# RWKV-7 chains of a hybrid diffusion layer: joins put between the steps of the preceding job's chain, states of two pairs updated side by side

## The chip, the cores and the metric

The kernel is one program on one core of one Trainium2 chip. Its engines are TensorE (PE, with its weight loads as PEld), VectorE (DVE), ScalarE (ACT), GpSimd (POOL) and SyncE (SP), which issues most of the DMAs. The metric is the device time in microseconds, and a lower one is better. Each engine works through its own list of instructions in order and waits on semaphores for the others.

## What is computed

The reference is one layer with two groups of heads. A chunkwise mLSTM and a bidirectional RWKV-7 read the same input projection, first for 256 context tokens and then for 512 latent tokens. The latent scans start from the context's final states. An output projection, a gated convolutional FFN and a norm follow.

```python
def rwkv7_scan(r, w, k, v, kk, a, s0, reverse):
    def step(s, xs):
        r_t, w_t, k_t, v_t, kk_t, a_t = xs
        s = (s * w_t[:, :, None, :]
             - jnp.einsum("bhvk,bhk->bhv", s, kk_t)[..., None] * (kk_t * a_t)[:, :, None, :]
             + v_t[..., :, None] * k_t[..., None, :])
        return s, jnp.einsum("bhvk,bhk->bhv", s, r_t)
...
y_f, s_f = rwkv7_scan(rh, hd(decay[:, :, 0]), ..., state[2], False)
y_b, s_b = rwkv7_scan(rh, hd(decay[:, :, 1]), ..., state[3], True)
```

There are 16 such heads of 64 channels, in two directions.

## The kernel before

**Stages.** First come the modulation vectors and the context tokens' input projection, done in parts. Then the latent tokens' input projection runs head by head: `x_first`, `x_pair(0)` to `x_pair(7)`, and the four `x_head`s. Then the output projection runs in two halves (`out_first` over channels whose inputs are ready early, then the rest), and the FFN follows. All projections are split into high and low parts: ACT writes `whi` (line 299), DVE writes `wlo` (line 300), and each tile of weights gives three matmuls (lines 370 to 372 for `proj`, 403 to 405 for `proj_tm`, 1266 to 1268 for the first half of the output projection).

**RWKV-7 in chunks.** Heads are handled as 8 pairs, and two pairs make a job: four jobs for the context (4 chunks of 64 tokens each) and four for the latent tokens (8 chunks each). I call the latent jobs A (pairs 0 and 1), B (2, 3), C (4, 5) and D (6, 7). A job goes through four parts:

- `prep` (lines 680 to 775), once per pair and direction for the latent tokens: decays, masked products of all chunks (`G`, line 750) and transposed keys (line 759), written to DRAM in `S_d`.
- `tsolve` (777 to 801): 60 operations on DVE, one after the other, that invert 32x32 triangular blocks.
- `tjoin` (803 to 827): joins these blocks to 64x64 ones. For each pair it loads `t_Y`, transposes on DVE (813), multiplies on PE (819), copies on ACT (821), multiplies again (824), copies on DVE (826) and stores. There is one buffer `t_Y`, so the second pair's load waits for the first pair's store. Its PSUM banks come from the pool "pre", which `prep` uses too.
- `chain` and `chain_step` (843 to 933): the recurrence over chunks, forward and backward for both pairs at once. That makes four units, each with a state `u.M` of 128x64. A step multiplies the values and the states with the chunk's matrices (line 868), copies the result to `r_Rs` on ACT (872), multiplies again (875, 878), copies to `r_U` on ACT (880), multiplies with that (884, 887), and then DVE makes the new states (892) and adds to the outputs `r_yt` (902, 904). All products of a step lie in two banks of the pool "R", which has two, so the next step's first products wait until DVE has read both.

**Order.** `x_job(p)` runs `prep` for pair p. If a job is solved it then joins it, if a job is joined it runs its chain, and after every second pair it solves the two just made. So the chain of A stands in `x_job(2)`, those of B and C in `x_job(4)` and `x_job(6)`, and D is joined and run through its chain behind the loop. Between two steps of a latent chain (at c = 2 and 6) `fin_step` takes up half a `finalize_pair`, the normalisation and gating of a pair whose chain is done. `ada_late` puts 4 MB chunks of the modulation weights through DVE (line 232). The mLSTM heads (`mlstm_head`) 0 to 2 use buffers of the pool `rp` that `prep`, `tsolve` and `tjoin` use as well (`t_X`, `r_Gp`, `r_KR`), so they can only start when the last pair's are free. This program order is a priority: the build reorders each engine's list by its own timeline, so that projections stand between the steps of the chains.

Of the kernel before, what the change touches and what calls it, by code (L numbers as in the profile page):

```python
# [96 lines left out]
def body(tc, A, dbg=None):  # L97
# [705 lines left out]
    def tjoin(pairs):  # L803

        nc_ = 2 * pairs[0][0].nch
        XT = rp("t_X", [P, 2, 16, 32], 1)
        for k, us in enumerate(pairs):
            kc = us[0].kc
            T_d = us[0].S_d[:, :, kc:kc + 64]
            T = rp("t_Y", [P, 16, 64], 1)[:, 0:nc_]  # L810
            sp.dma_start(T, T_d)
            W = XT[:, k, 0:nc_]
            dve.transpose(W, T[:, :, 0:32])
            ws = [PS("pre", [P, 16, 32])[:, 0:nc_] for _ in range(2)]
# [12 lines left out]
            sp.dma_start(T_d, T)  # L827

# [14 lines left out]
    def chain_step(units, first, last):  # L843
# [5 lines left out]
        opened = {}  # L849

# [12 lines left out]
        for src in (1, 0):  # L863
            for u, w, c, V, n in units:
                for j in range(2 if x else 1):
                    for h in range(2):
                        o = 2 * kc * src + 64 * j
                        mm(h, h if j == 0 else 1 - h, n, w[:, o:o + 64], V[:, c, :] if src else u.M)
# [4 lines left out]
        for u, w, c, V, n in units:  # L873
            for h in range(2):
                mm(h, 1 - h, 4 + n, w[:, kc:kc + 64], Rs[:, n, :])
            for h in range(2):
                if not last:
                    mm(h, h, 4 + n, w[:, 3 * kc + 64:3 * kc + 128], V[:, c, :])
        for h, hs in enumerate(LOHI):
            act.copy(U[hs], bank[h][LOHI[1 - h], 4:8, :])  # L880
        for u, w, c, V, n in units:
            for h in range(2):
                if not last:
                    mm(h, h, 4 + n, w[:, 3 * kc:3 * kc + 64], U[:, n, :])
# [3 lines left out]
        if not last:  # L888
            for u, w, c, V, n in units:
                g = u.g0 + c  # L890
                for h, hs in enumerate(LOHI):
                    dve.scalar_tensor_tensor(u.M[hs], u.M[hs], u.gC[hs, g:g + 1], bank[h][hs, 4 + n, :], ALU.mult, ALU.add)  # L892
        if x:
            for k in range(0, len(units), 2):
                cs = [units[k][2], units[k + 1][2]]
                lo, hi = min(cs), max(cs)
                y = units[k][0].y
                for h in range(2):
                    hs = LOHI[1 - h]
                    out = y[hs, lo:hi + 1:hi - lo, :]  # L900
                    if first:
                        dve.tensor_copy(out, bank[h][hs, k:k + 2, :])
                    else:
                        dve.tensor_tensor(out, bank[h][hs, k:k + 2, :], out, ALU.add)

    def chain(pairs, mid):
# [3 lines left out]
        Vs, ys = [], []  # L910
        for us in pairs:
            Vs.append(chain_v(us[0].p, us[0].seg, nch))
            ys.append(rk("r_yt", [P, 8, 64], 2) if x else None)
            for u in us:
                if not x:
                    Mst[(u.p, u.d)] = rk("r_M", [P, 64], 16)
                    pool.memset(Mst[(u.p, u.d)], 0.0)
                u.M = Mst[(u.p, u.d)]
        for c in range(nch):
            if x and c in (2, 6):  # L920
                mid()
            units = []
            for k, (us, V, y) in enumerate(zip(pairs, Vs, ys)):
                us[0].y = y
                for j, u in enumerate(us):
                    cu = nch - 1 - c if j else c
                    units.append((u, chain_load(u, cu), cu, V, 2 * k + (j if 2 * c < nch - 1 else 1 - j)))
            chain_step(units, c < nch // 2, x and c == nch - 1)
        if x:
            for us, y in zip(pairs, ys):  # L930
                y_d = us[0].y_d = DT("yr_d", [4, P, 128], 8)
                for h in range(2):
                    sp.dma_start(y_d[:, :, 64 * h:64 * h + 64].rearrange("a (b t) v -> t (a b) v", t=64), y[LOHI[1 - h]])

    def bonus(p, uf, ub, s):
# [8 lines left out]
        bo = rk("r_bo", [P, 8], 6)  # L944
# [69 lines left out]
    def ctx_part(H, k0, k1, part):  # L1014
        for n, (tag, (kind, *ts)) in enumerate(ctx_plan):
            if k0 == 0:
                if tag == "am":
                    if n % 2 == 0:
                        pair = am()
# [128 lines left out]

    def do_solve():
        job = list(made)  # L1150
        made.clear()
        tsolve([us for _, us, _ in job])
        solved.append(job)

    def ctx_job(p):
# [3 lines left out]
        do_join()  # L1159
        do_chain()  # L1160
        do_solve()

    def x_job(p):
# [4 lines left out]
        do_join()  # L1168
        do_chain()
        if p % 2:  # L1170
            do_solve()

# [69 lines left out]
    do_join()  # L1242
# [262 lines left out]
```

## Time and profile before

| what | value |
|---|---|
| time, median of 3 runs | 3369.24 us (3366.53 to 3373.36) |
| the profiled execution | 3371.52 us, its span 3369.7 us |
| PE busy | 3081.6 us (91%) |
| DVE busy | 2165.6 us (64%) |
| ACT busy | 1182.0 us (35%) |
| mean granted clock of TensorE | 0.938 |

The profile page gives busy times as shares of the whole span, which joins stages with different limits. So it is to be read by stages: from the table of stretches, which has one row per stretch with the busy time of each engine, the granted clock, the share of the DMA engines and what they moved. The FFN, from 1890 us on, is a stage of its own.

### The profile page before, as it was taken

The numbers are of one execution on the slowest core, as the hardware profiler recorded it, in microseconds if no ns is written. First come the engines' busy times: TensorE is split into PE (matmuls) and PEld (weight loads), VectorE is DVE, ScalarE is ACT, GpSimd is POOL, SyncE is SP. The second block draws the span as 40 slices with busy tenths as digits, with TensorE's granted clock in tenths as the row PEclk, the third lists the DMA queues.
The fourth block names the chain that finished last, engine by engine and source line by source line (L and its number), as shares of the span: only waits on it lengthen the run. The fifth ranks groups of instructions, "written<-read, shape, count | busy, mean of one in ns | idle before, by whom it ended". The sixth has DMA issues, their size and how long they took to land.

```text
span 3369.7 us, 54393 instructions
## 1 busy us (share of the span) xinstructions
PE 3081.6 (91%) x21030; PEld 2518.3 (75%) x21030; DVE 2165.6 (64%) x4178; ACT 1182.0 (35%) x2237; POOL 58.4 (2%) x113
## 2 busy tenths in 40 slices
PE   8998889898988989567898899999999999999998
PEld 5687777787876767445676688888888888888887
DVE  2578766669668796747744788455555555555657
ACT  4356444334343434214333432232222222322323
POOL 0000100000000000000000000000000000000000
PEclk9998998999998999567898999999999999999999
DMA  8877554558566868657844255232232232222232
GB/s 282 309 243 227 154 152 146 166 158 264 179 202 203 261 208 246 207 162 248 280 155 143 82 194 194 94 100 95 94 100 95 94 99 96 94 98 96 94 100 101
DMA packets 404114, 548.53 MB, mean 163 GB/s; under 512 B 153200, under 2 KB 274312, under 8 KB 403600
## 3 DMA queue, kind: packets, MB, share of 16 engines
q1 hardware_dynamic: 394208, 531.68, 49.7%
q10 hardware_dynamic: 9648, 13.37, 1.1%
q8 instruction: 166, 2.72, 0.3%
q14 instruction: 92, 0.75, 0.1%
HBM read 457.49 MB, written 87.47 MB: 162 GB/s over the span
## 4 chain that ended last, share of the span: by engine, by line
PE 48%; DMA 6%; DVE 5%; ACT 2%; issue 1%; SPq 1%; POOL 0%; DVEq 0%; ACTq 0%
PE acc L370 9%; PE acc L372 9%; PE acc L371 9%; PE acc L1380 5%; PE acc L1381 5%; PE acc L1382 5%; DMA am<-in_wmod 2%; PE acc L1266 1%; PE acc L1268 1%; PE acc L1267 1%; DVE adacc L232 1%; DMA x_d<-ev 1%; DMA wraw<-in_wdn 0%; DVE r_M L892 0%; PE R L861 0%
## 5 line engine op out<-in xcount | busy, mean ns | idle before, releaser
L299 ACT CAST whi<-wraw 128x512 fp32r<-128x512 f32 (+1 forms) x948 | 569.1, 604 | 1342.6 <-PE acc L371 701.8
L300 DVE TENSOR_TENSOR wlo<-wraw,whi 128x512 fp32r<-128x512 f32 (+1 forms) x948 | 626.8, 665 | 462.2 <-ACT whi L299 455.9
L372 PE MATMUL acc<-H,wlo 128*128 128x512 f32 x1920 | 757.2, 394 | 6.2 <-DVE wlo L300 6.2
L370 PE MATMUL acc<-H,whi 128*128 128x512 f32 x1920 | 760.2, 396 | 1.2 <-ACT upad L1321 0.5
L371 PE MATMUL acc<-H,whi 128*128 128x512 f32 x1920 | 755.5, 393 | 0.0
L372 PEld LDWEIGHTS acc<-H,wlo 128*128 128x128 f32 x1920 | 363.8, 189 | 85.7 <-DVE wlo L300 8.4
L370 PEld LDWEIGHTS acc<-H,whi 128*128 128x128 f32 x1920 | 363.3, 189 | 82.4 <-issue 3.6
L371 PEld LDWEIGHTS acc<-H,whi 128*128 128x128 f32 x1920 | 363.7, 189 | 77.9 <-issue 2.9
L1384 DVE SCALAR_TENSOR_TENSOR x<-acc,mod,x 128x512 f32<-128x512 f32 (+1 forms) x192 | 135.5, 706 | 222.0 <-PE acc L1382 222.0
L1328 DVE SCALAR_TENSOR_TENSOR f_cv<-upad,fvec,f_cv 128x512 f32<-128x512 f32 x352 | 263.5, 749 | 7.2
L1380 PE MATMUL acc<-fh,whi 128*128 128x512 f32 x640 | 253.2, 396 | 0.0
L1381 PE MATMUL acc<-fl,whi 128*128 128x512 f32 x640 | 253.1, 396 | 0.0
L1382 PE MATMUL acc<-fh,wlo 128*128 128x512 f32 x640 | 253.1, 396 | 0.0
L232 DVE SCALAR_TENSOR_TENSOR adacc<-am,csil,adacc 128x512 f32<-128x512 f32 x240 | 179.1, 746 | 45.9 <-DMA am<-in_wmod 43.5
L405 PE MATMUL acc<-wlo,H 128*128 128x256 f32 x512 | 155.0, 306 | 6.5 <-DVE wlo L300 6.5
L403 PE MATMUL acc<-whi,H 128*128 128x256 f32 x512 | 155.9, 305 | 3.1 <-ACT whi L299 3.1
L404 PE MATMUL acc<-whi,H 128*128 128x256 f32 x512 | 152.9, 299 | 0.0
L1382 PEld LDWEIGHTS acc<-fh,wlo 128*128 128x128 f32 x640 | 120.2, 188 | 29.1
L1381 PEld LDWEIGHTS acc<-fl,whi 128*128 128x128 f32 x640 | 120.2, 188 | 29.0
L1380 PEld LDWEIGHTS acc<-fh,whi 128*128 128x128 f32 x640 | 120.2, 188 | 29.0
L750 DVE TENSOR_TENSOR r_Gp<-pre,c_gmask 64x512 f32<-64x512 f32 (+1 forms) x192 | 115.1, 600 | 25.0 <-DMA Sx_d<-r_Gp 14.6
L1266 PE MATMUL acc<-H,whi 128*128 128x512 f32 x256 | 104.6, 413 | 22.4 <-ACT H L299 17.4
(350 smaller groups left out, 4686.5 us busy)
## 6 DMA issues: line engine op xcount, KB each, us to landing
am<-in_wmod SPq DMA_DIRECT2D x128, 512.0 KB
wraw<-in_wup SPq DMA_DIRECT2D x88, 512.0 KB
wraw<-in_wgate SPq DMA_DIRECT2D x88, 512.0 KB
wraw<-in_wdn SPq DMA_DIRECT2D x88, 512.0 KB
wraw<-in_wcm SPq DMA_DIRECT2D x72, 512.0 KB
r_GK<-Sx_d SPq DMA_DIRECT2D x128, 256.0 KB
wraw<-in_wtm SPq DMA_DIRECT2D x56, 512.0 KB
Sx_d<-r_Gp SPq DMA_DIRECT2D x32, 512.0 KB
```

Of the source, the lines that this page charges most:

```text
L232: dve.scalar_tensor_tensor(acc, wm[:, k % 2], csil[:, k:k + 1], acc, ALU.mult, ALU.add)
L299: act.copy(hi, t)
L300: dve.tensor_tensor(lo, t, hi.bitcast(F32), ALU.subtract)
L370: pe.matmul(pt[:, :n], hi(k8), H.h(k), start=k == 0, stop=False)
L371: pe.matmul(pt[:, :n], hi(k8), H.l(k), start=False, stop=False)
L372: pe.matmul(pt[:, :n], lo(k8), H.h(k), start=False, stop=k == KT - 1)
L403: pe.matmul(o, H.h(k)[:, xs], hi(k4), start=first, stop=False, skip_group_check=True)
L405: pe.matmul(o, H.h(k)[:, xs], lo(k4), start=False, stop=k == KT - 1, skip_group_check=True)
L1328: dve.scalar_tensor_tensor(cv, u[:, a:a + GH, b:b + GW], fvec[:, f, tap:tap + 1], cv, ALU.mult, ALU.add)
L1380: pe.matmul(pt, hi(m)[:, k, :], th[:, cs], start=k == 0, stop=False)
L1381: pe.matmul(pt, hi(m)[:, k, :], tl[:, cs], start=False, stop=False)
L1382: pe.matmul(pt, lo(m)[:, k, :], th[:, cs], start=False, stop=k == GF - 1)
```

## The change

It does six things.

- The joins no longer stand in one piece. `tjoin` becomes a generator that yields after each pair, and takes its banks from "R", the chain's pool. For a latent chain the two pairs of the next solved job are joined between its steps, at c = 4 and c = 5; for a context chain at c = 2 and 3. The first context job, which has no chain before it, is joined outright.
- The chain of a job now stands one job later: `x_job` with an odd p solves the two pairs just made and then runs the chain of the job before. So A's chain stands in `x_job(3)`, B's in `x_job(5)`, C's in `x_job(7)`, and D's behind the loop as before.
- The states of a job's four units lie side by side in one tile `M` of 128x4x64. What was one operation per unit and head is one per head: `Ms = M * gj` (one 128x256 product ahead of the step's matmuls) and `M = bank + Ms` (two operations of 64x256).
- The outputs of both pairs lie in one tile `y`, and are copied or added in one operation of 64x256 per head instead of two of 64x128.
- The decays are put in order for that by four copies on POOL per job (`r_gj`).
- `r_bo` gets two more buffers, and `r_yt` is one tile in place of two.

```diff
@@ tjoin @@
-            ws = [PS("pre", [P, 16, 32])[:, 0:nc_] for _ in range(2)]
+            ws = [PS("R", [P, 16, 32])[:, 0:nc_] for _ in range(2)]
...
             sp.dma_start(T_d, T)
+            yield
@@ chain_step @@
-    def chain_step(units, first, last):
+    def chain_step(units, M, gj, y, first, last):
...
+        Ms = rk("r_Ms", [P, 4, 64], 1)
+        if not last:
+            dve.tensor_tensor(Ms, M, gj[:, :, None].to_broadcast([P, 4, 64]), ALU.mult)
...
         if not last:
-            for u, w, c, V, n in units:
-                g = u.g0 + c
-                for h, hs in enumerate(LOHI):
-                    dve.scalar_tensor_tensor(u.M[hs], u.M[hs], u.gC[hs, g:g + 1], bank[h][hs, 4 + n, :], ALU.mult, ALU.add)
+            for h, hs in enumerate(LOHI):
+                dve.tensor_tensor(M[hs], bank[h][hs, 4:8, :], Ms[hs], ALU.add)
         if x:
-            for k in range(0, len(units), 2):
-                cs = [units[k][2], units[k + 1][2]]
-                lo, hi = min(cs), max(cs)
-                y = units[k][0].y
-                for h in range(2):
-                    hs = LOHI[1 - h]
-                    out = y[hs, lo:hi + 1:hi - lo, :]
-                    if first:
-                        dve.tensor_copy(out, bank[h][hs, k:k + 2, :])
-                    else:
-                        dve.tensor_tensor(out, bank[h][hs, k:k + 2, :], out, ALU.add)
+            cs = [units[0][2], units[1][2]]
+            lo, hi = min(cs), max(cs)
+            for h in range(2):
+                hs = LOHI[1 - h]
+                out = y[hs, :, lo:hi + 1:hi - lo, :]
+                src = bank[h][hs, 0:4, :].rearrange("p (a b) v -> p a b v", b=2)
+                if first:
+                    dve.tensor_copy(out, src)
+                else:
+                    dve.tensor_tensor(out, src, out, ALU.add)
@@ chain @@
-    def chain(pairs, mid):
+    def chain(pairs, hooks):
...
+        gj = rk("r_gj", [P, 8, 4], 2)
+        for k, us in enumerate(pairs):
+            for j, u in enumerate(us):
+                back = slice(None, None, -1) if j else slice(None)
+                pool.tensor_copy(gj[:, 0:nch, 2 * k + j], u.gC[:, u.g0:u.g0 + nch][:, back])
         for c in range(nch):
-            if x and c in (2, 6):
-                mid()
+            for f in hooks.get(c, ()):
+                f()
...
+    def join_step():
+        if solved:
+            job, stream = solved[0]
+            next(stream)
+            if next_pair.pop(0) == 1:
+                next_pair.extend((0, 1))
+                joined.append(solved.pop(0)[0])
+    next_pair = [0, 1]
     def do_chain():
-        if joined:
-            job = joined.pop(0)
-            chain([us for _, us, _ in job], fin_step)
-            fin_q.extend(t for t in job if t[2] is not None)
-
-    def do_join():
-        if solved:
-            job = solved.pop(0)
-            tjoin([us for _, us, _ in job])
-            joined.append(job)
+        if not joined:
+            join_step()
+            join_step()
+            return
+        job = joined.pop(0)
+        x = job[0][2] is not None
+        hooks = {2: [fin_step], 4: [join_step], 5: [join_step], 6: [fin_step]} if x else {2: [join_step], 3: [join_step]}
+        chain([us for _, us, _ in job], hooks)
+        fin_q.extend(t for t in job if x)
...
     def ctx_job(p):
...
-        do_join()
+        do_solve()
         do_chain()
-        do_solve()
     def x_job(p):
...
-        do_join()
-        do_chain()
         if p % 2:
             do_solve()
+            do_chain()
@@ behind the loop over pairs @@
-    do_join()
```

What becomes of this in the engines' lists shows at three places. The first is PE, around the last matmul of the latent input projection. Here is PE in before, 65 rows behind that last matmul. `r_U` and `r_V` are operands of the chain of job C, `R_12511`, `R_12512` and `R_12603` its banks; line 759 transposes and line 701 projects for `prep` of pair 7.

```order
L861 MATMUL R_12511<-r_U_12546,r_GK_12509 64x64
L861 MATMUL R_12512<-r_U_12546,r_GK_12509 64x64
L759 MATMUL pre_13419<-c_ident_90,r_cum_13417 128x128 x4
L701 MATMUL pre_13430<-r_lw_6615,r_up_13339 128x512
L858 MATMUL R_12603<-r_V_12495,r_GK_12595 64x64 x2
L861 MATMUL R_12603<-r_V_12495,r_GK_12597 64x64 x2
L861 MATMUL R_12603<-r_V_12499,r_GK_12599 64x64 x2
```

In before the first step of C ends here, behind the whole input projection, and `prep` of pair 7 is still to come in part, as are D's solve and join and all of D's chain. In after, PE's list has this at the end of the input projection: the last matmuls of the projection, and then job C's fifth step, from its copies `r_Rs` on.

```order
L370 MATMUL acc_16959<-H_2691,whi_17000 128x512
L371 MATMUL acc_16959<-H_2692,whi_17000 128x512
L372 MATMUL acc_16959<-H_2691,wlo_17001 128x512
L865 MATMUL R_13141<-r_Rs_13177,r_GK_13133 64x64
L865 MATMUL R_13141<-r_V_12669,r_GK_13133 64x64
```

Four steps of C and the join of D's first pair have gone ahead of this place. 22 rows further on, where that fifth step ends, stands the join of D's second pair (lines 819 and 824, in banks of "R") and the sixth step's first products.

```order
L865 MATMUL R_13142<-r_U_13178,r_GK_13139 64x64 x2
L819 MATMUL R_13222<-t_X_13058,t_Y_13219 32x32 x16
L819 MATMUL R_13223<-t_X_13058,t_Y_13219 32x32 x16
L824 MATMUL R_13222<-t_Y_13219,t_X_13058 32x32 x16
L824 MATMUL R_13223<-t_Y_13219,t_X_13058 32x32 x16
L862 MATMUL R_13301<-r_V_12669,r_GK_13293 64x64 x2
```

The join of a pair has moved from a place of its own to between two steps, and the banks it writes are those that the steps take in turn.

The second place is PE in after where the last product of `prep` and `bonus` for pair 7 stands (lines 759 and 945), with the latent input projection's matmuls (403 to 405) behind it.

```order
L865 MATMUL R_9820<-r_V_9137,r_GK_9817 64x64
L759 MATMUL pre_12568<-c_ident_90,r_cum_12566 128x128 x4
L945 MATMUL pre_12583<-r_rk_2282_12581,r_kd_12425 128x2 x4
L405 MATMUL acc_15091<-wlo_15215,H_2689 128x256
L403 MATMUL acc_15091<-whi_15214,H_2689 128x256
```

These rows are 6036 to 6041 of PE's list, some 1800 rows ahead of the projection's last matmul; in before the same rows stand behind it, so all of pair 7's `prep` has moved ahead.

The third place is DVE at the end of a step of C's chain, in before: the updates of the four states' lower halves and both pairs' outputs from the first of the step's banks.

```order
L892 SCALAR_TENSOR_TENSOR r_M_5735<-r_M_5735,r_gC_10142,R_13129 64x64
L892 SCALAR_TENSOR_TENSOR r_M_5737<-r_M_5737,r_gC_10230,R_13129 64x64
L892 SCALAR_TENSOR_TENSOR r_M_5742<-r_M_5742,r_gC_11708,R_13129 64x64
L892 SCALAR_TENSOR_TENSOR r_M_5744<-r_M_5744,r_gC_11796,R_13129 64x64
L904 TENSOR_TENSOR r_yt_12498<-R_13129,r_yt_12498 64x2x64
L904 TENSOR_TENSOR r_yt_12502<-R_13129,r_yt_12502 64x2x64
```

And in after, the end of a step of C, both banks:

```order
L894 TENSOR_TENSOR r_M_5782<-R_13141,r_Ms_13143 64x256
L905 TENSOR_TENSOR r_yt_12675<-R_13141,r_yt_12675 64x2x128
L894 TENSOR_TENSOR r_M_5782<-R_13142,r_Ms_13143 64x256
L905 TENSOR_TENSOR r_yt_12675<-R_13142,r_yt_12675 64x2x128
L853 TENSOR_TENSOR r_Ms_13303<-r_M_5782,r_gj_12676 128x256
```

Twelve operations have become four, and the next step's `r_Ms` comes behind them.

## Rows read from the trace of the kernel before

**Rows 1.** The profile page: span, busy shares, granted clock in 40 slices.

```profile
span 3369.7 us, 54393 instructions
...
PE 3081.6 (91%) x21030; PEld 2518.3 (75%) x21030; DVE 2165.6 (64%) x4178; ACT 1182.0 (35%) x2237; POOL 58.4 (2%) x113
...
PEclk9998998999998999567898999999999999999999
```

**Rows 2.** Stretches: start:end length, PE PEld DVE ACT POOL busy, clock, DMA, GB/s.

```profile
317.00:1327.00 1010.00, 906.68 (x8958) 757.08 (x8957) 744.92 (x1656) 415.17 (x830) 51.20 (x62) 0.93 0.64 191
1327.00:1400.00 73.00, 45.46 (x669) 37.69 (x670) 50.93 (x124) 24.97 (x56) 0.40 (x3) 0.61 0.75 244
1400.00:1487.00 87.00, 43.06 (x723) 37.29 (x719) 48.33 (x133) 13.98 (x28) 0.00 (x0) 0.50 0.52 144
1487.00:1655.00 168.00, 130.44 (x1282) 94.35 (x1281) 123.10 (x309) 65.33 (x163) 0.56 (x6) 0.81 0.82 266
1655.00:1788.00 133.00, 114.13 (x503) 93.49 (x501) 61.30 (x131) 38.93 (x86) 1.23 (x2) 0.93 0.58 190
1890.00:3369.00 1479.00, 1461.71 (x6564) 1204.36 (x6564) 894.39 (x1371) 429.48 (x711) 0.00 (x0) 1.00 0.32 107
```

**Rows 3.** Timeline of PE: start, duration, operation, count, [idle before, what ended it].

```profile
1327.26 0.39 PE L372 MATMUL acc<-H,wlo 128*128 128x512 f32 x1
...
1337.19 1.61 PE L861 MATMUL R<-r_U,r_GK 64*64 64x64 f32 x32
...
1348.91 1.27 PE L861 MATMUL R<-r_U,r_GK 64*64 64x64 f32 x32 [2.72 <-ACT r_U L880]
...
1474.37 0.49 PE L858 MATMUL R<-r_V,r_GK 64*64 64x64 f32 x8 [10.81 <-DMA r_GK<-Sx_d]
...
1482.41 5.54 PE L605 MATMUL pre<-r_kr,r_KR 128*128 128x512 f32 x8
...
1787.67 0.80 PE L1266 MATMUL acc<-H,whi 128*128 128x512 f32 x1 [10.55 <-ACT H L299]
```

**Rows 4.** Timeline of ACT: `r_Rs` of C's first and last steps, D's first and last.

```profile
1330.20 0.76 ACT L872 COPY r_Rs<-R 64x256 f32<-64x256 f32 x2 [1.62 <-PE R L861]
...
1441.77 0.37 ACT L872 COPY r_Rs<-R 64x256 f32<-64x256 f32 x1 [5.91 <-PE R L861]
...
1499.15 0.76 ACT L872 COPY r_Rs<-R 64x256 f32<-64x256 f32 x2 [0.58 <-PE R L861]
...
1638.25 0.35 ACT L872 COPY r_Rs<-R 64x256 f32<-64x256 f32 x1
```

**Rows 5.** Timeline of DVE: D's solve begins and ends, join's transposes of both pairs.

```profile
1392.82 0.20 DVE L798 TENSOR_TENSOR t_T<-t_X 128x30 f32<-128x30 f32 x1 [6.29 <-DMA t_X<-Sx_d]
...
1444.50 0.19 DVE L799 TENSOR_TENSOR t_X<-t_X,t_T 128x30 f32<-128x30 f32 x1
...
1457.11 0.71 DVE L813 STREAM_TRANSPOSE t_X<-t_Y 128x512 f32<-128x512 f32 x1 [9.23 <-DMA t_Y<-Sx_d]
...
1473.57 0.71 DVE L813 STREAM_TRANSPOSE t_X<-t_Y 128x512 f32<-128x512 f32 x1 [8.60 <-DMA t_Y<-Sx_d]
```

**Rows 6.** Timelines, DVE then PE: C's first step ends, second step's first products.

```profile
1338.91 1.96 DVE L892 SCALAR_TENSOR_TENSOR r_M<-r_M,r_gC,R 64x64 f32<-64x64 f32 x8
1340.79 1.23 DVE L902 COPY r_yt<-R 64x128 f32<-64x128 f32 x4
...
1341.80 0.48 PE L858 MATMUL R<-r_V,r_GK 64*64 64x64 f32 x4
```

**Rows 7.** Groups by shape on DVE: xcount | busy us, mean ns | idle before.

```profile
L232 DVE SCALAR_TENSOR_TENSOR adacc<-am,csil,adacc 128x512 f32<-128x512 f32 x240 | 179.1, 746 | 45.9 <-DMA am<-in_wmod 43.5
...
L750 DVE TENSOR_TENSOR r_Gp<-pre,c_gmask 64x256 f32<-64x256 f32 x64 | 27.0, 422 | 7.1 <-PE pre L747 3.7 <-DMA Sc_d<-r_Gp 2.1 <-PE R L861 0.2
```

**Rows 8.** Groups on POOL: copies of decays.

```profile
L721 POOL COPY r_gC<-r_E 128x4 f32<-128x4 f32 (+1 forms) x32 | 46.2, 1451 | 1092.0 <-ACT r_E L720 1092.0
```

More of the change, by code (lines that the diff above doesn't have):

```diff
@@ L863, in chain_step @@
         for src in (1, 0):
-            for u, w, c, V, n in units:
+            for u, w, c, V, n, m in units:
                 for j in range(2 if x else 1):
@@ L872, in chain_step @@
             act.copy(Rs[hs], bank[h][hs, 0:4, :])
-        for u, w, c, V, n in units:
+        for u, w, c, V, n, m in units:
             for h in range(2):
@@ L908, in chain @@
         x = pairs[0][0].seg == "x"
         nch = pairs[0][0].nch
[L910 to L918, printed above, removed]
+        key = pairs[0][0].p
+        Vs = [chain_v(us[0].p, us[0].seg, nch) for us in pairs]
@@ L919, in chain @@
+        y = rk("r_yt", [P, 2, 8, 64], 1) if x else None
+        if not x:
+            Mst[key] = rk("r_M", [P, 4, 64], 4)
+            pool.memset(Mst[key], 0.0)
+        gj = rk("r_gj", [P, 8, 4], 2)
[3 more added lines that the diff above has]
+                pool.tensor_copy(gj[:, 0:nch, 2 * k + j], u.gC[:, u.g0:u.g0 + nch][:, back])
         for c in range(nch):
-            if x and c in (2, 6):
-                mid()
+            for f in hooks.get(c, ()):
+                f()
@@ L922, in chain @@
             units = []
-            for k, (us, V, y) in enumerate(zip(pairs, Vs, ys)):
-                us[0].y = y
+            for k, (us, V) in enumerate(zip(pairs, Vs)):
                 for j, u in enumerate(us):
                     cu = nch - 1 - c if j else c
-                    units.append((u, chain_load(u, cu), cu, V, 2 * k + (j if 2 * c < nch - 1 else 1 - j)))
-            chain_step(units, c < nch // 2, x and c == nch - 1)
+                    units.append((u, chain_load(u, cu), cu, V, 2 * k + (j if 2 * c < nch - 1 else 1 - j), 2 * k + j))
@@ L929, in chain @@
+            chain_step(units, Mst[key], gj[:, c, :], y, c < nch // 2, x and c == nch - 1)
         if x:
-            for us, y in zip(pairs, ys):
+            for k, us in enumerate(pairs):
                 y_d = us[0].y_d = DT("yr_d", [4, P, 128], 8)
                 for h in range(2):
-                    sp.dma_start(y_d[:, :, 64 * h:64 * h + 64].rearrange("a (b t) v -> t (a b) v", t=64), y[LOHI[1 - h]])
+                    sp.dma_start(y_d[:, :, 64 * h:64 * h + 64].rearrange("a (b t) v -> t (a b) v", t=64), y[LOHI[1 - h], k])
@@ L943, in bonus @@
             pe.matmul(pb[:, tt, :], kd[:, 128 * tt:128 * tt + 128], rk2, start=True, stop=True)
-        bo = rk("r_bo", [P, 8], 6)
+        bo = rk("r_bo", [P, 8], 8)
         act.copy(bo, pb.rearrange("p a b -> p (a b)"))
@@ L1016, in ctx_part @@
             if k0 == 0:
-                if tag == "am":
+                if tag in ("am", "r_yt"):
                     if n % 2 == 0:
-                        pair = am()
+                        pair = am() if tag == "am" else rk("r_yt", [P, 2, 512], 1)
                     d = pair[:, n % 2]
@@ L1151, in do_solve @@
         made.clear()
-        tsolve([us for _, us, _ in job])
-        solved.append(job)
+        pairs = [us for _, us, _ in job]
+        tsolve(pairs)
+        solved.append((job, tjoin(pairs)))
     def ctx_job(p):
```

9 lines of the change are left out of this document (4 added, 5 removed).

## The prediction, as it was put on record

> **What bounds the kernel now.** I read the page first [rows 1]: TensorE is busy for 91% of the span, and the row of granted clocks falls to 5 in one place only, a little behind the middle. Then the table of stretches [rows 2], which takes the kernel apart. The FFN behind 1890 us has PE busy for 1461.71 of 1479 us at clock 1.00: nothing of it is touched, and I take it as it stands. The latent input projection from 317 to 1327 us has PE busy for 906.68 of 1010 us (90%) at 0.93, so there work decides, not waiting. Between 1327 and 1655 us it is the other way round: PE is busy for 45.46 of 73, 43.06 of 87 and 130.44 of 168 us, at clocks of 0.61, 0.50 and 0.81. No engine is full there. Something serial sets the time, and the timelines say what.
>
> The timeline of PE shows the last projection matmul at 1327.26 [rows 3]. Job C's first `r_Rs` comes at 1330.20 and its eighth at 1441.77, seven intervals of 15.9 us; job D's come from 1499.15 to 1638.25, seven of 19.9 us [rows 4]. Between the two chains stand the end of D's solve on DVE (1392.82 to 1444.50) and D's join, whose second pair's transpose comes 16.5 us behind the first's, after a wait of 8.60 us for its load [rows 5]. So 16 chain steps and a join lie bare behind the projection, 311 us from 1327.26 to the last `r_Rs`. Behind that 149 us pass until the second half of the output projection starts at 1787.67 [rows 3, 4], most of it PE work (114.13 of 133 us busy from 1655 to 1788) [rows 2].
>
> **The change part by part.** *Chain and join moved.* In the changed kernel's list for PE, four steps of C, the values' and states' products of the fifth, all of pair 7's `prep`, D's solve and the join of D's first pair stand ahead of the last projection matmul. Behind it remain the rest of C's fifth step, three more of C, eight of D and one pair's join. Counted from that fifth `r_Rs` to D's last, that is 11 intervals where before had 16 steps, a solve and a join.
>
> What is an interval worth? C's 15.9 us were taken beside `prep` and a slow clock, D's 19.9 beside the mLSTM heads; the remaining 11 are of both sorts, so I start from their mean, 17.9. From this comes what the merged updates save. In before DVE needs from 1338.91 to 1342.02, 3.11 us, until a step's states and outputs are out of its banks, and the next step's first product is at 1341.80 [rows 6]. After, four operations of 64x256 do this; the nearest row of that shape on the same engine takes 422 ns [rows 7], so 1.69 us: 1.42 less. The new product `Ms` (128x256, one more of 422 ns) needs only the old states and lies beside PE's work; if it falls on the path the gain is 1.0. I take 1.1, and 16.8 us an interval. The tail up to D's last `r_Rs` becomes a join, which between 0 and its bare 16.5 us [rows 5] I put at 7, plus 11 x 16.8 = 185, together 192 in place of 311: **-119 us**. The bounds: between the output products of C's first and second steps, 1337.19 and 1348.91, only 11.7 us pass [rows 3], which gives 7 + 129 = 136 (-175); with 19.9 us each it is 226 (-85).
>
> *What this puts into the projection.* The moved work must be done there. By the stretches, 1327 to 1400 holds C's first steps and the rest of `prep`: 45.46 us of PE at clock 0.61 are 27.7 us at full clock [rows 2]. Half a join and the modulation sums that come ahead are some 4.5 us of the following stretch (43.06 x 0.50 = 21.5 for the rest of the chain and two joins), and head 0's first products 2.8 (5.54 at half clock) [rows 2, 3]. That is 35 us, at the stage's density of 0.90: **+40 us** to the stage's end, which comes at 1367. Below it can't fall far, since PE there has only 103 us of idle time in all: if the moved steps fill holes, 15. Above: if PE is half idle beside them, as from 1400 to 1487 (43.06 of 87 us busy), 80. DVE does not become the bound: it is busy for 744.92 of 1010 us there [rows 2]; three more modulation chunks of 15 operations of 746 ns [rows 7] add 34 us, the solve, `prep` and steps about 40, and the merged updates take about 42 off.
>
> *Behind the chain.* At D's last step 60 more matmuls' worth (512 columns each) of the output projection have been done in the changed list, some 14 us of PE, so that the stretch up to the second half shrinks by as much: **-14** (0 to -20).
>
> *Edits costed at nothing.* The copies of decays are four per job on POOL, 1.45 us each by the nearest copy [rows 8], 46 us in all; POOL is busy for 58.4 us of the whole span [rows 1] and the decays are ready from `prep`, a job earlier. Without that cover it is 5.8 us a job. The matrices' loads, the transfers of outputs and the number of PE's products stay the same. The joins' loads and stores now stand in SP's queue between the loads of the chain's matrices: a store that waits for DVE's copies holds back the next step's `r_GK`. Before has a PE wait of 10.81 us ended by `r_GK` in the midst of the join [rows 3]; here that cost lies in the 7 us, and in a rival.
>
> The sum: -119 + 40 - 14 = -93 us. The profiled execution took 3371.5, so 3278.5; the median lies 2.3 below it, so **3276 us**.
>
> **The rivals.** *The joins lie bare between the steps.* There is one buffer for a join's blocks, and the join takes the two banks that the next step needs. If each pair's join costs the whole 16.5 us [rows 5], the tail is 9.5 us longer, and in the projection five pairs (both of B, both of C, D's first) cost up to 82, where PE waits in order with matmuls queued behind: up to 3276 + 92 = 3368, no change. For it speaks the 10.81 us wait [rows 3]; against it that the build has put projection matmuls between most joins and their next step, and that before's joins stood there too while the stage kept its 90%. That part of it holds gives 3300 to 3345.
>
> *A denser tail.* With the solve and joins gone, PE could go on at a higher clock and set the time by work: 27.7 + 21.5 + 0.81 x 130.44 + 0.93 x 114.13 = 261 us of full-clock work lay between 1327 and 1788 [rows 2]; less 35 it is 226, at a density of 0.90 about 250 us, so the second half would start at 1367 + 250 = 1617 and not at 1695: 3200.
>
> *Slower: the chains' waits stop the projection.* Twenty latent steps (A, B and four of C) now stand among the projections, where PE works in order, so a wait for `r_U` stops the matmuls behind it. In the bare chain PE waits 2.72 us for `r_U` [rows 3] and 5.91 for PE's own products before `r_Rs` on ACT [rows 4]. To end slower by 0.2%, 100 us of the gain must go back, which is 5.0 us of new idle time in each step; at 7.7 (an interval of 15.9 less 8.2 of PE work at half clock) it would be 154, and the time 3430. Against it: 16 of those steps stood among projections before, and all idle time of the stage was 103 us [rows 2], so only the four new ones can well cost that much.
>
> *A rule against merging.* The next step's first product starts only when both banks have been read: 1341.80 beside outputs that end at 1342.02 [rows 6]. Here splitting would free nothing sooner. The Trainium skill, page "Perfetto Trace Analysis", section "Optimizing Scalar/DVE Operations", says otherwise: "If Scalar/Vector aren't saturated, but are causing bubbles on other engines, breaking up instructions may allow work to be completed sooner." By that rule the merge would be worth nothing or less. If the merge saves nothing, the interval stays 17.9, the tail is 12 us longer, and the time 3288: inside the range, with a chance of 0.15 within the forecast's. *The change doing less than it says* (the reordered list runs, but the chain of D isn't what the output waits for) is the same as a tail that keeps its length: 3276 + 119 = 3395; the wait of 10.55 us for `H` ahead of 1787.67 [rows 3] speaks against it, and I give it no more than 0.02.
>
> **How the numbers follow.** Chances: the forecast, 3215 to 3300, 0.62; joins partly bare, 3300 to 3345, 0.18; joins wholly bare, 3345 to 3375, 0.07, most of it within 0.2%; the dense tail below 3215, 0.06; slower, by stopped projections 0.05 or an unmoved tail 0.02. Range 3215 to 3345, which leaves out 0.20. The measurement tells about 0.2% (6.7 us) from no change. Faster: 0.62 + 0.18 + 0.06 + 0.02 = 0.88; the same 0.05; slower 0.07.
>
> **What would show it.** In the changed kernel's trace: the last projection matmul near 1367 (right if 1340 to 1390); four `r_Rs` of C ahead of it and twelve behind, 16.8 us apart; the last at about 1559; the output's second half from about 1695; the clock in the tail at 0.7 or more in place of 0.5. The forecast is wrong if the projection's end comes later than 1407, if intervals stay at 20 us or grow since the mLSTM heads now share the time with C as well as D, or if a join's load and store stand as an idle PE of 10 us or more between two steps at more than one place.

## The result and the profile after

The changed kernel takes 3246.26 us (median of 4 runs, 3244.45 to 3250.93) against 3371.02 of before on the same chip; the ratio of the two is 0.9634, with a 95% interval of 0.9617 to 0.9650. That is 125 us less. The prediction was 3276 us, 93 us less, with a range of 3215 to 3345.

The profiled execution took 3247.18 us. First the profile page of the changed kernel, the lines that answer to [rows 1]:

```profile
span 3245.4 us, 54082 instructions
...
PE 3045.4 (94%) x21030; PEld 2483.8 (77%) x21030; DVE 2121.9 (65%) x3894; ACT 1156.4 (36%) x2216; POOL 75.9 (2%) x133
...
PEclk9998999999998999887999999999999999999999
```

PE has the same 21030 matmuls and DVE 284 instructions less. The place of low clock has shrunk: the row falls to 7 and not to 5. Now the table of stretches, which answers to [rows 2] (start:end length, then the busy times of PE, PEld, DVE, ACT and POOL, the granted clock, the DMA share, GB/s):

```profile
317.00:1355.00 1038.00, 940.80 (x9790) 778.86 (x9788) 810.50 (x1679) 441.91 (x892) 67.40 (x93) 0.95 0.73 217
1355.00:1425.00 70.00, 53.95 (x676) 42.31 (x675) 34.13 (x84) 24.42 (x68) 0.21 (x2) 0.74 0.62 180
1425.00:1544.00 119.00, 103.73 (x1156) 77.65 (x1155) 86.83 (x188) 40.29 (x107) 0.35 (x4) 0.77 0.84 276
1544.00:1664.00 120.00, 105.79 (x506) 87.33 (x506) 52.57 (x117) 28.43 (x78) 1.24 (x2) 0.96 0.59 183
1766.00:3245.00 1479.00, 1461.65 (x6563) 1204.08 (x6562) 892.72 (x1368) 428.51 (x709) 0.00 (x0) 1.00 0.32 107
```

The FFN is as long as before, 1479 us. The projection now ends at 1355 instead of 1327, and behind it the second half of the output projection starts after 309 us instead of 460. Busy time times clock makes the two kernels comparable. From 317 us to that start before did 843 + 28 + 22 + 106 + 106 = 1104 us of full-clock work in 1471 us [rows 2], the changed kernel 894 + 40 + 80 + 102 = 1115 in 1347. So the work is the same within 1%, and it is done at 0.83 of full speed instead of 0.75.

Four rows of its timelines answer to [rows 3, 4]. On PE, the last projection matmul and the first of the output's second half:

```profile
1354.81 0.39 PE L372 MATMUL acc<-H,wlo 128*128 128x512 f32 x1
...
1664.27 0.79 PE L1276 MATMUL acc<-H,whi 128*128 128x512 f32 x1 [9.46 <-ACT H L299]
```

And on ACT, the `r_Rs` of C's fifth step and of D's last:

```profile
1352.53 0.76 ACT L876 COPY r_Rs<-R 64x256 f32<-64x256 f32 x2 [0.89 <-PE R L865]
...
1543.95 0.76 ACT L876 COPY r_Rs<-R 64x256 f32<-64x256 f32 x2 [2.52 <-PE R L865]
```

C's fifth step is at the projection's very end, as forecast, and eleven intervals of 17.4 us lead from it to D's last step.

And the last masked products of pair 7's `prep`, on DVE, in before:

```profile
1381.62 2.80 DVE L750 TENSOR_TENSOR r_Gp<-pre,c_gmask 64x512 f32<-64x512 f32 x4 [3.53 <-DMA Sx_d<-r_Gp]
```

and in the changed kernel:

```profile
1092.61 2.81 DVE L750 TENSOR_TENSOR r_Gp<-pre,c_gmask 64x512 f32<-64x512 f32 x4 [1.86 <-DMA Sx_d<-r_Gp]
```

`prep` is done 289 us earlier. The experiments show that the order's gain hangs on the change of banks that goes with this move; that change by itself is worth 38 of the 125 us.

### The profile page after: what moved, and what is told of

It is laid out like the page before. It is cut to its first block, busy times and chain, and to the rows that moved or that the text cites. A ratio compares the mean times of both kernels' runs of the same rounds, so it can differ in the third digit from the quotient of the medians.

```text
span 3245.4 us, 54082 instructions
## 1 busy us (share of the span) xinstructions
PE 3045.4 (94%) x21030; PEld 2483.8 (77%) x21030; DVE 2121.9 (65%) x3894; ACT 1156.4 (36%) x2216; POOL 75.9 (2%) x133
## 4 chain that ended last, share of the span: by engine, by line
PE 66%; DMA 13%; DVE 12%; issue 3%; ACT 3%; SPq 2%; POOL 0%; DVEq 0%; ACTq 0%
PE acc L372 10%; PE acc L370 10%; PE acc L371 10%; PE acc L1390 5%; PE acc L1391 5%; PE acc L1392 5%; DMA am<-in_wmod 2%; PE R L865 2%; DVE wlo L300 2%; PE pre L195 2%; DVE r_Gp L750 2%; PE acc L1276 2%; PE acc L1277 1%; PE acc L1278 1%; DVE adacc L232 1%
```

## The experiments

Theory A is that of the prediction: what counts is how many chain steps lie bare behind the projection. I first took the change apart. The ratios are against the kernel before, run beside each.

**The merged updates alone**, in before's order. `r_yt`, `M` and `chain_step` are those of the changed kernel, the hooks those of before:

```diff
-            chain([us for _, us, _ in job], fin_step)
+            chain([us for _, us, _ in job], {2: [fin_step], 6: [fin_step]} if job[0][2] is not None else {})
```

> The order of before, with the states and outputs of two pairs side by side and updated as in the changed kernel. Theory A (the gain is chain steps that no longer lie bare behind the projection; a bare step costs about 17 us, one among the projections about 4 to 5): in the built list 14 steps of C and D still stand behind the last projection matmul where before had 15 and a half, and each is 1.1 us shorter, so the tail loses about 35 us and the projection gains 5: about 3340 us. Rival B (the merged updates make the gain, since every step waits for DVE): 3270 or less, most of the 125 us.

Measured: 0.9852 (0.9838 to 0.9867), 50 us less. That is more than Theory A's 30 and far from Rival B's 90 and over. The last `r_Rs` comes 269 us behind the projection's end instead of 311, the projection ends 4 us earlier, and 14 steps instead of 16 are left behind it.

**The order alone**, with old updates:

```diff
-            for h, hs in enumerate(LOHI):
-                dve.tensor_tensor(M[hs], bank[h][hs, 4:8, :], Ms[hs], ALU.add)
+            for u, w, c, V, n, m in units:
+                g = u.g0 + c
+                for h, hs in enumerate(LOHI):
+                    dve.scalar_tensor_tensor(M[hs, m, :], M[hs, m, :], u.gC[hs, g:g + 1], bank[h][hs, 4 + m, :], ALU.mult, ALU.add)
```

> The order of the changed kernel, with one update of the state per unit and head and one of the outputs per pair and head, as in before. Theory A: 12 steps and both joins of D stand behind the last projection matmul, where the changed kernel has 11 and a half and one join; about one bare step (17), half a join (8) and 1.1 us for each of 11 steps more than the changed kernel: about 3283 us. Rival B (the merged updates make the gain): above 3330.

Measured: 0.9758 (0.9741 to 0.9775), 3280.6 us, as Theory A had it, and not above 3330 as Rival B had it. The two parts add up: 0.9852 x 0.9758 = 0.9614, against 0.9634 for both. So the merge is worth some 1.3 to 1.5%, the order 2.2 to 2.4%.

**Joins between the steps, but in `prep`'s banks.**

```diff
-            ws = [PS("R", [P, 16, 32])[:, 0:nc_] for _ in range(2)]
+            ws = [PS("pre", [P, 16, 32])[:, 0:nc_] for _ in range(2)]
```

> The changed kernel with one word undone: the joins between the steps take their banks from the pool of prep again. In the built list prep of pair 7, both joins of C and D and 18 steps then stand behind the last projection matmul (11 and a half steps and one join in the changed kernel). Theory A: 6 to 7 more bare steps at 12 us each net, three more joins at 10 to 16 and a solve: about 130 to 160 us over the changed kernel, 3375 to 3405, so the whole gain is gone. Rival C (the gain comes from the chain standing one job later, whatever the banks): below 3290.

Measured: 1.0230 (1.0215 to 1.0245), 3440 us: one word turns a gain of 125 us into a loss of 77. Theory A had the sign and two thirds to four fifths of the size (130 to 160 us over the changed kernel, where 200 were measured). The stretches of this kernel, up to the projection's end at 1250 us and behind it:

```profile
317.00:1250.00 933.00, 862.71 (x8232) 713.00 (x8230) 636.16 (x1299) 387.81 (x772) 30.23 (x80) 0.96 0.61 187
1250.00:1490.00 240.00, 119.70 (x1762) 96.88 (x1760) 158.24 (x338) 63.54 (x134) 5.76 (x13) 0.57 0.57 165
```

The projection ends 105 us earlier than in the changed kernel, since less stands among it; behind it PE is half idle for 240 us, at clock 0.57. Pair 7's `prep` has its last masked products at 1444:

```profile
1444.03 2.79 DVE L750 TENSOR_TENSOR r_Gp<-pre,c_gmask 64x512 f32<-64x512 f32 x4 [4.27 <-DMA Sx_d<-r_Gp]
```

**Joins in one piece behind the chain**, in the chain's banks.

```diff
-        hooks = {2: [fin_step], 4: [join_step], 5: [join_step], 6: [fin_step]} if x else {2: [join_step], 3: [join_step]}
+        hooks = {2: [fin_step], 6: [fin_step]} if x else {}
         chain([us for _, us, _ in job], hooks)
+        join_step()
+        join_step()
```

> The changed kernel with each job's joins in one piece behind the preceding chain instead of between its fourth to sixth steps. In the built list 15 steps and both joins of D lie behind the last projection matmul. Theory A: four more bare steps at 12 us net, and one more join of 8 to 16 us: about 3246 + 60 = 3306. Rival C (the chain one job later is what counts, not where the joins stand): within 10 us of 3246.

Measured: 0.9749 (0.9732 to 0.9765), 3281.8 us: 39 us worse than the changed kernel (0.0115 of 3363), where Theory A had 60 and Rival C 10. This kernel has 16 `r_Rs` behind a projection that ends at 1325 us, just like before, and yet it is 81 us faster than before; the merged updates are some 42 to 50 of these. So the number of bare steps alone can't be what counts. C's steps are 10.4 us apart on average here instead of 15.9. Pair 7's `prep` is done at 1091 us and no longer runs beside them, as it did in before until 1384; D's solve still runs beside the first of them, until 1353. That it is `prep` that made the difference is argued from this, not shown by itself. C's first, fifth, sixth and eighth step:

```profile
1326.04 0.37 ACT L876 COPY r_Rs<-R 64x256 f32<-64x256 f32 x1
...
1371.92 0.37 ACT L876 COPY r_Rs<-R 64x256 f32<-64x256 f32 x1 [10.11 <-PE R L865]
...
1378.43 0.37 ACT L876 COPY r_Rs<-R 64x256 f32<-64x256 f32 x1 [3.26 <-PE R L865]
...
1398.76 0.37 ACT L876 COPY r_Rs<-R 64x256 f32<-64x256 f32 x1 [5.29 <-PE R L865]
```

(Each step has two such copies, one a head; these are the first of each. Single intervals go from 6.5 to 13.7 us.)

**The chain one job later and nothing else**, from the kernel before.

```diff
     def x_job(p):
...
-        do_join()
-        do_chain()
         if p % 2:
             do_solve()
+            do_chain()
+            do_join()
```

> The kernel before with its chains one job later and nothing else (joins in one piece behind the preceding chain, in the banks of prep; old updates; the two more buffers of r_bo that this order needs). In the built list 23 steps and two jobs' joins stand behind the last projection matmul, where before has 16 steps and one. Theory A (what counts is how many steps lie bare behind the projection): seven more bare steps at 10 to 16 us net of 4 to 6 saved in the projection, one more join of 16 to 30: 3363 + 60 to 130, about 3450. Rival C (the chain one job later is the gain): below 3330.

Measured: 1.0419 (1.0403 to 1.0434), 3505 us, slower by 142 us. Theory A had 60 to 130, and Rival C's gain is not there.

**The same with the joins in the chain's banks** (the word above, the other way round).

> The same with the joins' banks from the chain's pool, still in one piece and with the old updates. In the built list 18 steps and both joins of C and D lie behind the last projection matmul, but prep of pair 7 ahead of it. Theory A: two more bare steps than before (+25) and a second join (+20), less prep out of the tail (some 40 to 60, by the run with joins behind the chain, where C's steps were 10.4 us apart instead of 15.9): 3363 + 0, between 3335 and 3385. Rival C: below 3330, since the order is that of the changed kernel but for the place of the joins.

Measured: 0.9911 (0.9894 to 0.9927), 3333.6 us, 30 us less than before, just under the range that Theory A gave and just over Rival C's bound; by itself it decides nothing. The one word is worth 171 us here, in the order that was worst without it.

**A step more among the projections, a step more behind them.** Here the outputs and later states are not the reference's, since one step is done three times.

```diff
-        for c in range(nch):
-            for f in hooks.get(c, ()):
+        for c in [0, 1, 2, 3, 4, 5, 5, 5, 6, 7] if x and key == 0 else range(nch):
+            for f in hooks.pop(c, ()):
```

> The changed kernel with two steps more in job A (its sixth step is done three times, so outputs and later states differ from the reference), among the projections. Theory A (a step among projections costs its PE work and little more, some 4 to 7 us, plus what it pushes out behind the projection; in the built list half a step and half a join more lie there): 10 to 30 us over the changed kernel, about 3262 on the chip of the first result. Rival D (the chains are one serial thread, so each step costs the same wherever it stands, 17 us): 35 us.

Measured: 0.9690 (0.9676 to 0.9704), 19 us over the changed kernel, within Theory A's 10 to 30 and not Rival D's 35. With `key == 6`, job D:

> The changed kernel with two steps more in job D (its sixth step is done three times), bare behind the projection. Theory A: 2 x 17.4 us, less what runs beside them, 25 to 35 us over the changed kernel: about 3277. Rival E (the tail is set by PE's work in it, not by the chain): 8 us or less, the work of two steps.

Measured: 0.9658 (0.9639 to 0.9677), 8 us over the changed kernel, with an interval that overlaps its own. Theory A falls: its 25 to 35 us are not there, although 15 `r_Rs` lie behind the projection here and 11 in the changed kernel (two more of C's steps had slipped there too). Rival E had 8 us or less. D's last `r_Rs` in this run, on ACT, and then the start of the output's second half, on PE:

```profile
1567.42 0.76 ACT L876 COPY r_Rs<-R 64x256 f32<-64x256 f32 x2 [0.21 <-PE R L865]
```

```profile
1664.61 1.22 PE L1276 MATMUL acc<-H,whi 128*128 128x512 f32 x2 [6.04 <-ACT H L299]
```

The projection's last matmul is at 1347.69 here, 7 us earlier than in the run of the changed kernel. Counted from there the chain's end has moved by 31 us (1567.42 - 1347.69 = 220 against 189), the output's second half by 7 (317 against 309). So in the changed kernel the chain of D does not set the end. I formed another theory, H: it is the mLSTM heads, which begin when D's join gives their buffers free, in one of two forms: heads follow each other, or TensorE's work is the limit.

**D's join earlier, or later, with the chain as it is.**

```diff
+        if x and job[0][0] == 4:
+            hooks = {0: [join_step], 1: [join_step], 2: [fin_step], 6: [fin_step]}
```

> The changed kernel with D's join put between the first steps of C's chain (c = 0 and 1) instead of the fourth to sixth; all else, the steps' number and the other jobs' joins, as it was. In the built list D's join ends ahead of the last projection matmul, and head 1's first products stand there too; as many chain steps lie behind it as in the changed kernel. Theory A (the chain's bare steps set the end): no gain, 3240 +- 8 on this chip. Theory H (from the end of D's join on, heads 0 to 3 follow each other for some 300 us whatever the chain does; the join gives their buffers free): the join ends 40 to 55 us earlier, and of this 20 to 45 us come through: 3195 to 3220.

Measured: 0.9615 (0.9592 to 0.9637), 6 us under the changed kernel and not told apart from it. D's join is done at 1305 us instead of 1365. Its last copies on DVE, in the changed kernel and then in this run:

```profile
1364.19 0.69 DVE L826 COPY t_Y<-R 32x512 f32<-32x512 f32 x1 [0.85 <-PE R L824]
```

```profile
1304.05 1.40 DVE L826 COPY t_Y<-R 32x512 f32<-32x512 f32 x2 [1.16 <-PE R L824]
```

And with `{2: [fin_step], 4: [join_step], 6: [fin_step], 7: [join_step]}`:

> The changed kernel with the join of D's second pair between the seventh and eighth step of C instead of the fifth and sixth; the lists are the same up to there. Theory H: the join ends 25 to 35 us later and the time goes with it: 3265 to 3275. Theory A: only the first step of D waits for the join, some 5 to 12 us: 3245 to 3252.

Measured: 0.9650 (0.9623 to 0.9676), 5 us over, unclear too; the join is done at 1389, 24 us later:

```profile
1388.29 0.69 DVE L826 COPY t_Y<-R 32x512 f32<-32x512 f32 x1 [0.85 <-PE R L824]
```

The serial form of Theory H falls: 60 us earlier and 24 us later both leave the time where it was, within 6 us. Theory A's figures for these two runs (3240 +- 8 and 3245 to 3252) were met, so the two do not speak against it; the run with two steps more in D does. With the early join the projection itself ends 65 us later, at 1419.78, and the output's second half starts 23 us earlier, at 1641.21, of which 8 us are lost again behind it.

**A head done twice.**

```diff
                 run([mlstm_head(i, True)])
+                if i == 1:
+                    run([mlstm_head(i, True)])
```

> The changed kernel with mLSTM head 1 done twice, the same values stored again, behind the projection. Theory A (the chain of D is the path, heads fill its waits): less than 20 us. Theory H in its serial form (heads follow each other): one head's spacing, 50 us. Theory H in its other form (behind the join TensorE's work at the granted clock is the limit): a head has 24 us of PE work at full clock, which at the tail's 0.72 (busy share times clock) is 33 us.

Measured: 0.9725 (0.9698 to 0.9752), 31 us over the changed kernel; the second form of Theory H had 33. Its stretches, from where the changed kernel's projection ends (this one's ends at 1349.7 us) to the output's second half:

```profile
1355.00:1425.00 70.00, 55.99 (x636) 44.01 (x638) 34.83 (x85) 21.34 (x64) 0.21 (x2) 0.72 0.61 182
1425.00:1544.00 119.00, 101.71 (x1163) 77.25 (x1158) 73.90 (x178) 45.33 (x129) 0.55 (x6) 0.80 0.71 224
1544.00:1694.00 150.00, 127.88 (x557) 101.69 (x555) 76.53 (x159) 35.92 (x96) 1.24 (x2) 0.93 0.64 209
```

That is 40.3 + 81.4 + 118.9 = 240.6 us of full-clock work in 339 us, 0.71; the changed kernel did 221 in 309, 0.72. So the tail grew as its work did, at about the same density. The run does not single TensorE out, though: head 1 done again adds busy time on DVE and ACT too (some 15 and 13 us), and heads that follow each other and overlap in part are not excluded.

Nor is 0.72 a property of every tail. Here are the same stretches, from the projection's end to the output's second half, with the joins in one piece:

```profile
1325.00:1703.00 378.00, 302.88 (x3027) 245.56 (x3026) 208.01 (x476) 102.20 (x276) 1.79 (x8) 0.77 0.63 201
```

and with D's join early:

```profile
1420.00:1641.00 221.00, 193.32 (x1773) 146.60 (x1771) 130.56 (x275) 64.97 (x160) 1.34 (x3) 0.90 0.66 213
```

These are densities of 0.62 and 0.79; before has 0.54. What the runs show is that near the changed kernel added work lengthens the tail at 0.72, and a longer chain or a moved join does not; what sets the density they do not show.

By the same count two chain steps are some 7 us of work at full clock (in the row below, 51.95 us at 0.76 for the 11 steps behind the projection), which is 10 us at 0.72, where 8 was measured (give or take about as much, by the two intervals). The row is of line 865, the chain's matmuls, of the changed kernel:

```profile
1355.00:1544.00 189.00, 51.95 (x1288) 47.26 (x1288) 0.76 0.76 240
```

**The one word alone.** This left the banks. In the nine kernels above with joins in "R", the changed one among them and whatever their order, the last masked products of pair 7's `prep` end between 1084 and 1128 us; in the four with "pre", before among them, between 1353 and 1497. (The text on record below speaks of four of them.) So the last run is the kernel before with that word changed and nothing else.

```diff
-            ws = [PS("pre", [P, 16, 32])[:, 0:nc_] for _ in range(2)]
+            ws = [PS("R", [P, 16, 32])[:, 0:nc_] for _ in range(2)]
```

> The kernel before with one word changed: the joins take their banks from the chain's pool instead of prep's. Theory B1 (prep's products queue behind the joins for banks of one pool, and joins behind chains; the other pool sets prep free): prep of pair 7 ends near 1100 us instead of 1384, as in all four runs with joins in the chain's banks (1091 to 1106 us), and D's solve is done by some 1300; PE's work moves ahead of the projection's end and the time falls by 30 to 70 us, to 3295 to 3335, although in the built list 16 steps and two jobs' joins lie behind the projection. Theory A (the number of steps left behind the projection counts): 16 as in before and one job's joins more, so 3365 to 3395.

Measured: 0.9886 (0.9869 to 0.9904), 38 us or 1.1% less than before, within Theory B1's range, and Theory A's 3365 to 3395 falls again. D's solve was not done by 1300, as Theory B1 had it, but at 1383. `prep` is done at 1113 us, by its last masked products on DVE; behind that row, the stretch that follows the projection's end (1322):

```profile
1110.16 2.80 DVE L750 TENSOR_TENSOR r_Gp<-pre,c_gmask 64x512 f32<-64x512 f32 x4 [2.20 <-DMA Sx_d<-r_Gp]
```

```profile
1326.00:1450.00 124.00, 68.55 (x1295) 62.95 (x1294) 56.77 (x184) 16.53 (x43) 0.00 (x0) 0.50 0.51 134
```

C's eight steps, the join of C's second pair and that of D's first are still bare there, at clock 0.50 (the lower of its two levels throughout), so only a part of the 125 us is had.

## Why the prediction was right, point by point

**The time** came out 30 us below the forecast, inside the range, and the direction was right. The terms of the sum against the trace: the projection's end, +40, measured +28 (1327.26 to 1354.81); the tail up to D's last `r_Rs`, -119, measured -122 (311 to 189); what follows up to the output's second half, -14, measured -29 (149 to 120). Half of the 30 us is that third term, most of the rest the first. The third was mis-sized: 45 more matmuls of the output projection stood ahead of D's last step (93 against 48), not 60, and yet it was twice the forecast. Its stretch was also worked through more densely: busy share times clock is 0.85 there (105.79 of 120 us at 0.96) and 0.80 in before (129.71 of 150 us at 0.92).

Three slips of the working cost little. The 35 us are full-clock work, but the 0.90 that they were divided by is a busy share; with the clock of 0.93 it is 0.83, and the term +42. The upper bound with PE half idle is then 35 / 0.495 = 71 and not 80. And the wait of 5.91 us is ACT's, for PE's products, not PE's [rows 4].

**What held.** Before's tail had half-idle engines at a low clock, and the order that takes `prep`, the solve, a join and four steps of C into the projection is the greater part of the gain (82 us alone). That the projection has room for it held more than forecast: PE is busy there for 940.80 of 1038 us at 0.95, so 50 us of full-clock work went in for 28 us of time, where the forecast had 35 for 40. Joins between the steps are worth having: 39 us against joins in one piece. The rival of joins that lie wholly bare did not come: from C's first step to D's last, PE's longest idle time is 8.35 us (a wait for `r_U`, at 1399.46), so the sign of 10 us and more between steps is absent too.

**The step that failed is the price of a step in the tail.** "11 x 16.8 us", with 7 for the join, met the measured 11 x 17.4, in which the join is contained, for another reason than the one given: that this term came out is luck. An interval of the changed kernel's tail isn't what a step needs from its waits: with little beside it, a step takes 10.4 us on average (joins behind the chain), and two more of them cost 8 us together, not 34. Other work stands between the steps on PE: from 1355 to 1544 us it is busy for 158 us, and the chain's line 865 for 52 of these. So the rival "a denser tail" was right on the work (226 us, measured 221) and nearer to what the runs show, and wrong on the density, 0.72 and not 0.90; it gave 3200. The forecast took the means of two intervals that other work had stretched and read them as a property of the chain.

**The merge was mis-sized.** I had 1.1 us in 11 intervals, 12 us. It measured 50 us alone and 42 on top of the order. The price of one operation was near: the new updates take 420 and 422 ns, as the row of that shape had said. What it saves in a step depends on the place. With the merge alone D's steps are 1.8 us closer than before's. But where C has little beside it, its steps are 10.4 us apart with the merged updates (joins in one piece) and with the old ones (the one word alone). What I left out are the steps among the projections: with the merge alone two more of C's get ahead of the projection's end, and on top of the order the merge brings that end 20 us forward, to 1354.81 from 1374.67 (in an execution of the order alone that took 10 us more than its median). That those steps got shorter is inferred. Groups by shape on DVE, in the changed kernel:

```profile
L894 DVE TENSOR_TENSOR r_M<-R,r_Ms 64x256 f32<-64x256 f32 x88 | 37.0, 420 | 14.7 <-PE R L865 12.8
L853 DVE TENSOR_TENSOR r_Ms<-r_M,r_gj 128x256 f32<-128x256 f32 x44 | 18.3, 416 | 0.3
```

The rule against merging, in the Trainium skill's page "Perfetto Trace Analysis", section "Optimizing Scalar/DVE Operations", says that breaking up "may" help, and has the measurement against it here: fewer, longer operations on an engine that was busy for 64% made the kernel 1.5% faster.

**The banks stood in the wrong place of the argument.** I counted the joins' move into "R" as a possible cost (they take the two banks that the next step needs). It is the condition of the gain: with the joins in "pre" the same change is 2.3% slower than before, and alone the move is worth 1.1%. That `prep` moves with this word is shown. That it moves because the joins and `prep` take the banks of one pool in turn, so that a pair's `prep` stands behind joins that stand behind a chain, is inferred from the lists and the times of `prep`; a run with more banks was not made, and other users of "pre" (the heads, the modulation sums) were not told apart from `prep`. The Trainium skill, page "Perfetto Trace Analysis", section "Optimization Strategy", says that a gap that repeats for a stretch, on the engine that should be full, can mean that there isn't enough SBUF or PSUM for the next tile. Before's largest wait of PE in the projection looks like one: line 759 reads no `r_Gp`, so what it waits for is probably a bank of "pre" that line 750 still reads.

```profile
PE pre L759 <- DVE r_Gp L750: 24.9, 10, 5.0
```

(In total 24.9 us, ten times, 5.0 at the longest.) But that is `prep` waiting for itself, and the changed kernel has 31.0 us of it. No product of `prep` is shown there waiting for a copy of the join (lines 821, 826); only the run with one word changed shows what the joins' banks cost.

**Left open.** What holds the tail at 0.72 of full speed: the clock of 0.74 to 0.77 up to 1544 us is a good part of it, and no run tried to raise it. How the merge's 42 to 50 us come about is known in part. Neither of the two other places of D's join was told apart from the changed kernel.

## What to carry to other kernels

A pool of banks that a feeding stage shares with the step behind it (here `prep` with the join) can tie the feeding stage to a recurrence that it does not depend on; here one word that gave the join other banks was worth 38 us in one order and 171 in another, and the order that was made for it paid only with it. An interval between steps that is read where other work runs beside is not the price of a step: add two steps and measure. And where several serial pieces lie behind a full engine, work out that engine's busy time times its clock over the stretch first: near the changed kernel, work added there cost time, and chain steps added there hardly any.

## What the runs showed of the chip

The granted clock stays low over long stretches in which PE is by no means idle: with only the bank changed, 0.50 from 1326 to 1450 us, with PE busy for 68.55 of 124 us, against 0.74 in the 70 us behind the changed kernel's projection, with PE busy for 53.95. And a low clock need not go with long steps of the chain: at 0.50 and 0.54, in two kernels where C's chain has little beside it, its steps are 10.4 us apart, while before's D took 19.9 us each at 0.81 beside the heads [rows 2, 4]. What a bare step would take at the full clock no run here shows; its products of line 865 are some 3.6 us of work at full clock (51.95 us at 0.76 for 11 steps), so an estimated 7 of the 10.4 at half of it. I had expected a slow clock to show in the chain first.
